# Gathers moved amid an expert pair's gate/up products, wider value products in two attention stages, and a later overflow loop in a hybrid decoder block

## The chip, the cores and the metric

The kernel runs on one core of a Trainium2 chip. A core has five engines with instruction streams of their own: TensorE (PE: matrix products and transposes), VectorE (DVE), ScalarE (ACT), GpSimd (POOL) and SyncE (SP, which here issues nearly all DMA transfers), and 16 DMA engines that move data between HBM and the on-chip memory SBUF. Products land in PSUM, eight banks of 2 KB a partition. Engines wait for one another on semaphores.

The metric is the device time of one execution in microseconds (us); lower is better.

## The reference

One decoder layer in float32, 512 tokens of width 1024, batch 1. Cut to what the change touches:

```python
h = rmsnorm(x, g_mix); proj = h @ w_in        # q, k, v of GLA and of MoBA, gates
o_g = gla_chunked(...)                        # 4 heads
o_m = moba_attention(q_m, k_m, v_m, rel_bias) # 8 heads of 64: softmax(q k^T + bias) @ v, causal
x = x + (sigmoid(z_g) * (o_g @ w_proj_gla) + sigmoid(z_m) * (o_m @ w_proj_moba)) @ w_out
k, v = split(mem_n @ w_ckv)                   # 256 memory tokens, 4 heads
x = x + memory_attention(rmsnorm(x, g_cross), mem_n, w_cq, w_ckv, w_co)
# hier_moe: 32 experts, each token goes to the top 2 of 8 in its best group
hid = silu(xb @ w_gate[e]) * (xb @ w_up[e])   # 1024 -> 512
out[token] += w * (hid @ w_down[e])           # 512 -> 1024
x = x + out; return rmsnorm(x, g_final)
```

Every expert is computed for up to 64 tokens at a fixed place; tokens beyond that go through a loop whose number of rounds is known only at run time. For these inputs it is zero.

## The kernel before

**Precision.** Most products keep float32 accuracy by splitting both operands into a high and a low part of 32 bits that TensorE takes in one pass; `mm3` issues three matmuls (high by high, low by high, high by low). `mm` is a single call; with plain float32 operands it leaves two records in the trace for each call. `wnext` hands out the next load of a weight list, split into high and low on ScalarE (L212) and VectorE (L213); a load is 512 KB.

**Ahead of the experts.** The input products run in the order of the list `plan`. `in_feat` makes features by tokens (`fo`), `in_rows` tokens by features (`ro`): for GLA's values `vg`, MoBA's values `vm`, and the memory's values `vc`. `in_rows` is called twice for each of them, for 256 columns at a time, with two loads a call of four 128-row parts each, and ScalarE evicts each tile of 128 tokens. The input products are woven with the GLA branch (`project`, `weave`). Then MoBA is woven with the gate projections (`gates`, the fill): for each of 16 items (four head pairs `hp` by four query tiles `i` of 128) the two scores `s_ps`; the values `mo_ps` of the item before; some fill; the softmax's end on VectorE (`normalise`); more fill; and the transposes of the probabilities (`ptp`, copied by ScalarE to `pt`). The table `FILL` says how much fill stands in either gap. `values` makes 2 (i + 1) products for the item, each 128 queries wide, onto 64 columns of the array for one head and the other 64 for the other.

**The experts.** 16 pairs of experts, p = 0 to 15. The pair's code runs for k = 0 to 7 `gate_up` (four calls, 128 by 64 tiles, two experts side by side), then `hidden` (silu on ScalarE, L1228; its product with up and the weight on VectorE, L1229), `hidden_t` (four transposes and a copy), and `down` for four parts, then `rows_hilo` splits the result. Between `hidden` and `down` stand the combine of the pair before (`c_ps`: 16 calls that add its results to the tokens' rows) and a part of a gather. `gather` picks the tokens of four experts, that is of two pairs, with a 0/1 matrix `oh` (`group_hots`, VectorE) in eight steps k of eight products (`g_ps`, 128 by 128 tiles), each evicted by ScalarE into `xT`; pair 2g − 2 runs four of these steps and pair 2g − 1 the other four, so all of a group's features are there before its first pair starts. `slot_rows` makes the matrix and the weights of the combine from the token codes that `c_bcast` copies to all partitions, by 16 transposes (`cb_ps`) amid pair 0.

**Loads of expert weights.** 384 loads of 512 KB, 24 a pair, into 48 buffers of one pool (`blk`, shared with `xT`, `oh` and others), issued by SP in order by `eload(n)`, which issues up to load n. A load waits until the products that read its buffer's last content are done, and no more than eight are under way. In pair p the kernel asks for 24 p + `DEPTH` loads at the start, two more behind every second k, and two more behind each part of `down`; `D0` gives the same for pair 0, and `elimit` holds the last 16 back until the loop has been passed.

**The loop.** `overflow` stands ahead of pair 15. It reads its round count into a register of every engine (L1266) and is entered and left through a barrier of all engines (L1268), also for zero rounds.

**The end.** The final norm works per tile of 128 tokens in two halves: VectorE makes the right, ScalarE (L1389) the left, and SP issues both output transfers (L1388, L1390).

## Time and profile before

| | us |
|---|---|
| three runs | 985.1, 985.75, 986.44 (median 985.75) |
| profiled execution, its own time | 985.1 |
| its span in the trace | 983.3 |
| TensorE busy | 961.1 |
| stages: projections and GLA | to about 183 |
| MoBA with the gates | 183 to 302 |
| merge, memory attention, routing | to 499.89 |
| expert pairs, to the end of the last down product | 499.89 to 969.5 |
| last combine, final norm, output | to 983.3 |

The profile is one execution. Its page gives the share of each engine, the stage windows the same for a stretch, with DMA rate and the granted clock of TensorE (1.00 is the higher of its two levels), and the timelines single instructions. A TensorE record's duration is longer than its share of the engine, since records overlap: what one costs is the step from its start to the next one's.

### The profile page before, as it was taken

What the parts mean: (1) busy time and instruction counts of PE and PEld (TensorE: products, weight loads), DVE (VectorE), ACT (ScalarE), POOL (GpSimd) and SP (SyncE); (2) the same over time, 40 slices, a digit from 0 to 9 for tenths busy, and PEclk for the clock granted to TensorE, in tenths of its full rate; (3) what the DMA queues carried; (4) which work ended last, traced back from release to release, by engine and by line L of the source; (5) the groups of instructions that cost most, each with busy time, mean ns of one, the idle gap of its engine ahead of it and who ended that gap; (6) DMA issues with size and microseconds to landing.
All of it is one profiled execution on the core that took longest, in us unless ns stands there. A gap on an engine that the chain in (4) does not pass through costs nothing. (4 is left out here: it accounts for less than half of the span.)

```text
span 983.3 us, 13899 instructions
## 1 busy us (share of the span) xinstructions
PE 961.1 (98%) x5305; PEld 645.5 (66%) x5305; DVE 474.8 (48%) x1048; ACT 311.7 (32%) x631; POOL 32.7 (3%) x46
## 2 busy tenths in 40 slices
PE   9999999999999999999999999999999999999985
PEld 7889779888788888999844555544555554455432
DVE  6343863345555746566752543434453333444314
ACT  5452633445446424455521111111111111111003
POOL 3200010000000000000000000000000000000003
PEclk9999999999999999999999999999999999999998
DMA  9512347133133522644588999999999999999993
GB/s 300 160 44 58 71 65 193 44 86 86 60 133 129 176 81 67 198 190 196 200 331 329 409 408 409 409 409 408 409 409 409 409 408 409 409 409 409 409 383 148
DMA packets 117161, 252.52 MB, mean 257 GB/s; under 512 B 10310, under 2 KB 61795, under 8 KB 117092
## 3 DMA queue, kind: packets, MB, share of 16 engines
q1 hardware_dynamic: 117092, 251.60, 69.3%
q8 instruction: 43, 0.70, 0.3%
q14 instruction: 26, 0.21, 0.1%
HBM read 247.90 MB, written 3.67 MB: 256 GB/s over the span
## 5 line engine op out<-in xcount | busy, mean ns | idle before, releaser
L136 PE MATMUL gu_ps<-we,xT 128*64 128x512 f32 x1024 | 229.3, 597 | 5.1 <-PEq L1268 3.8
L136 PEld LDWEIGHTS gu_ps<-we,xT 128*64 128x64 f32 x1024 | 78.0, 138 | 150.5 <-issue 134.6
L213 DVE TENSOR_TENSOR wlo<-wraw,whi 128x1024 fp32r<-128x1024 f32 (+1 forms) x71 | 86.6, 1238 | 90.0 <-ACT whi L212 89.8
L136 PE MATMUL y_ps<-we,hid_t 128*64 128x512 f32 x512 | 114.2, 595 | 0.3 <-issue 0.3
L1229 DVE SCALAR_TENSOR_TENSOR hid<-hid,ws,gu_ps 128x512 f32<-128x512 f32 x16 | 11.9, 747 | 194.9 <-PE gu_ps L136 194.9
L1262 DVE TENSOR_TENSOR x<-c_ps,x 128x512 f32<-128x512 f32 x120 | 76.7, 685 | 38.9 <-PE c_ps L136 38.9
L131 PE MATMUL fo<-hTh,whi 128*128 128x512 f32 x224 | 90.5, 404 | 0.0
L133 PE MATMUL fo<-hTh,wlo 128*128 128x512 f32 x224 | 87.5, 391 | 0.0
L132 PE MATMUL fo<-hTl,whi 128*128 128x512 f32 x224 | 87.4, 390 | 0.0
L136 PEld LDWEIGHTS y_ps<-we,hid_t 128*64 128x64 f32 x512 | 36.3, 137 | 68.8 <-issue 55.7
L212 ACT ACTIVATE whi<-wraw 128x1024 fp32r<-128x1024 f32 (+2 forms) x73 | 74.5, 1043 | 1.9 <-DMA wraw<-in_w_in_dram 1.8
L1228 ACT ACTIVATE hid<-gu_ps 128x512 f32<-128x512 f32 x16 | 9.6, 597 | 197.5 <-PE gu_ps L136 197.5
L136 PE MATMUL g_ps<-oh,xrh 128*128 128x256 f32 x256 | 64.6, 293 | 1.7 <-DVE oh L1030 1.7
L136 PE MATMUL g_ps<-oh,xrl 128*128 128x256 f32 x256 | 61.6, 281 | 0.0
L136 PEld LDWEIGHTS g_ps<-oh,xrh 128*128 128x128 f32 x256 | 47.0, 189 | 14.9 <-PE gu_ps L136 9.7
L133 PE MATMUL ro<-whi,hTl 128*128 128x256 f32 (+1 forms) x192 | 55.4, 289 | 0.8 <-DVE hTl L333 0.8
L131 PE MATMUL ro<-whi,hTh 128*128 128x256 f32 (+1 forms) x192 | 56.0, 291 | 0.0
L132 PE MATMUL ro<-wlo,hTh 128*128 128x256 f32 (+1 forms) x192 | 55.5, 289 | 0.2 <-POOL wlo L213 0.2
L212 ACT ACTIVATE yh<-y_ps 128x512 fp32r<-128x512 f32 x32 | 19.1, 598 | 109.9 <-PE y_ps L136 109.9
L136 PE MATMUL c_ps<-yh,ot 128*128 128x512 f32 x128 | 50.8, 397 | 0.7 <-ACT yh L212 0.7
L136 PE MATMUL c_ps<-yl,ot 128*128 128x512 f32 x128 | 50.8, 397 | 0.2 <-DVE yl L213 0.2
L131 PEld LDWEIGHTS fo<-hTh,whi 128*128 128x128 f32 x224 | 42.0, 188 | 12.0 <-issue 3.9
(320 smaller groups left out, 1544.5 us busy)
## 6 DMA issues: line engine op xcount, KB each, us to landing
we<-in_w_exp_gate_dram SPq DMA_DIRECT2D x128, 512.0 KB, 10.2
we<-in_w_exp_up_dram SPq DMA_DIRECT2D x128, 512.0 KB, 10.2
we<-in_w_exp_down_dram SPq DMA_DIRECT2D x128, 512.0 KB, 10.2
wraw<-in_w_in_dram SPq DMA_DIRECT2D x38, 512.0 KB, 3.8
wraw<-in_w_out_dram SPq DMA_DIRECT2D x8, 512.0 KB, 6.1
wraw<-in_w_ckv_dram SPq DMA_DIRECT2D x8, 512.0 KB, 4.6
wraw<-in_w_proj_gla_dram SPq DMA_DIRECT2D x4, 512.0 KB, 3.9
wraw<-in_w_proj_moba_dram SPq DMA_DIRECT2D x4, 512.0 KB, 4.3
```

Source lines behind the costliest of these rows:

```text
L131: PE.matmul(o, lh, rh, start=first, stop=False)
L132: PE.matmul(o, lh, rl, start=False, stop=False)
L133: PE.matmul(o, ll, rh, start=False, stop=last)
L136: PE.matmul(o, l, r, start=first, stop=last, **kw)
L212: S.activation(hi, src, AF.Copy)
L213: eng.tensor_tensor(lo, src, f(hi), op=ALU.subtract)
L1228: S.activation(row, gu[0][0:n], AF.Silu)
L1229: V.scalar_tensor_tensor(row, row, ws[:, 0:1], gu[1][0:n], op0=ALU.mult, op1=ALU.mult)
L1262: V.tensor_tensor(xs, o, xs, op=ALU.add)
```

## The change

- **Value rows 512 wide.** `in_rows` makes all 512 columns in one call, with four loads of two 128-row parts (`WIDE`) of the same size in place of two calls of two loads. Half the products, twice as wide; half the evictions, twice as wide.
- **MoBA values a head pair at a time.** `values(hp, pts)` runs once per head pair, behind the first scores of the next one, over all query tiles: for key tile j the queries from j on, 512, 384, 256 and 128 wide. `transposed` writes the probabilities of all four query tiles into two buffers a head, `pa` and `pb`, with one or two ScalarE copies a head.
- **The start.** The mean square of the second input tile moves from VectorE to ScalarE, into the gap that `to_feat` leaves for `between`.
- **`c_bcast`.** Its first two steps, the eight transposes of the codes, run ahead of the second half of the last gather before pair 0; the other two amid pair 0.
- **The gather.** A group's first four steps run behind the gate/up products of the odd pair ahead of it (p = 2g − 1), the other four amid the gate/up of its own first pair (p = 2g), one ahead of each k = 0 to 3. `xT` is taken from the pool in two halves; `group_hots` moves to k = 3 of the odd pair. Pair 0 runs no gather now and pair 14 runs four steps.
- **Loads.** `DEPTH` is 35 in pair 0 and 33 after it; `D0` is gone.
- **The loop.** The round count is read at the start of pair 14, and the loop stands in pair 15 ahead of k = 2 (`SPILL`); 372 loads are issued before it rather than 368. Inside it, products use one set of PSUM banks, `sp_ps`.
- **The end.** ScalarE issues the left halves' output transfers.

The diff, cut to its core:

```diff
-    def in_rows(n, evac, src, nt=NT, mark=None):
-        acc = [ps(f"ro{t}", [n]) for t in range(nt)]
-        for kh in range(2):
-            wh, wl = wnext(4, n)
+    def in_rows(evac, src, nt=NT, mark=None):
+        acc = [ps(f"ro{t}", [512]) for t in range(nt)]
+        kk = 0
+        for kn in WIDE:
+            wh, wl = wnext(kn, 512)
             for t in range(nt):
...
-    r1 = rms_scale(x_in[1], V)
-    to_feat(xr, hT, 0, lambda: wsplit(2))
+    def between():
+        r1.append(rms_scale(x_in[1]))
+        wsplit(2)
+    to_feat(xr, hT, 0, between)
...
-        def values(hp, i, pts, o_ps):
-            for j in range(i + 1):
+        def values(hp, pts):
+            o_ps = ps("mo_ps", [T])
+            for j in range(NT):
                 for half in range(2):
                     h = 2 * hp + half
                     sl = slice(64 * half, 64 * half + 64)
-                    mm(o_ps[sl, tcol(i)], vm[j][:, h * 64:(h + 1) * 64], pts[half][:, j, :], j == 0, j == i,
-                       skip_group_check=True)
+                    pa, pb = pts[half]
+                    p_j = pa[:, j, j * P:] if j < 2 else pb[:, j - 2, (j - 2) * P:]
+                    mm(o_ps[sl, j * P:], vm[j][:, h * 64:(h + 1) * 64], p_j, j == 0, j == NT - 1, skip_group_check=True)
...
             res = scores(hp, i)
-            if prev:
-                finish(*prev)
+            if prev and i == 0:
+                values(*prev)
...
+    bcast = c_bcast()
+    steps(bcast, 2)
     c_weights()
     c_gather(NT - 1)
...
-        if p == NP - 1:
-            eload(elimit[0])
-            overflow(*spilled)
-            elimit[0] = 12 * NE
-        eload(used + D0[0] if p == 0 else used + DEPTH)
-        if p % 2 == 0 and p:
-            xT = xT_next
+        depth = DEPTH[min(p, 1)]
+        if p == SPILL[0] - 1:
+            n_extra = nc.values_load(spilled[0][0:1, 0:1], ...
+        eload(used + depth)
         gu = [ps("gu_ps", [512]) for q in range(2)]
         s0 = (p % 2) * P
         for k in range(KD):
+            if (p, k) == SPILL[0:2]:
+                overflow(n_extra, *spilled)
+                elimit[0] = 12 * NE
+            if p % 2 == 0:
+                steps(gat, 1)
             gate_up(gu, k, [xT[k][:, s0 + CAP * i:s0 + CAP * i + CAP] for i in range(2)], w)
             if k % 2:
-                eload(D0[1 + k // 2] if p == 0 else used + DEPTH + 2 * (k + 1))
+                eload(used + depth + 2 * (k + 1))
...
+            if p % 2 and p + 1 < NP and k == OH_AT:
+                oh_next = group_hots((p + 1) // 2)
-        if p % 2 == 0 and p + 2 < NP:
-            xT_next = rows2("xT", KD, 4 * CAP)
-            gat = gather(oh_next, xT_next, 4 * CAP)
+        if p % 2 and p + 1 < NP:
+            xT = []
+            gat = gather(oh_next, xT, 4 * CAP)
...
-        gs = 4 if p + 2 < NP else 0
+        gs = 1 if p % 2 and p + 1 < NP else 0
...
-        SY.dma_start(out[tcol(t), 0:512], xg[t])
+        S.dma_start(out[tcol(t), 0:512], xg[t])
...
-SPILL_AT = 8
+WIDE = 2, 2, 2, 2
+SPILL = 15, 2, 372
...
-DEPTH = 30
-D0 = 34, 37, 41, 44, 47
+DEPTH = 35, 33
+OH_AT = 3
```

How the order moves, at three places. First TensorE's stream from the end of pair 1's down products into pair 2, before (`y_ps` down, `gu_ps` gate/up, `g_ps` gather, 16 calls leave 32 records):

```order
L136 MATMUL y_ps<-we,hid_t 64x512 x16
L136 MATMUL gu_ps<-we,xT_5124 64x512 x16
L136 MATMUL gu_ps<-we,xT_5125 64x512 x16
L136 MATMUL g_ps<-oh,xrh_4067 128x256
L136 MATMUL g_ps<-oh,xrl_4071 128x256
L136 MATMUL g_ps<-oh,xrh_4068 128x256
L136 MATMUL g_ps<-oh,xrl_4072 128x256
L136 MATMUL g_ps<-oh,xrh_4069 128x256
L136 MATMUL g_ps<-oh,xrl_4073 128x256
L136 MATMUL g_ps<-oh,xrh_4070 128x256
L136 MATMUL g_ps<-oh,xrl_4074 128x256
```

and after:

```order
L136 MATMUL y_ps<-we,hid_t 64x512 x16
L136 MATMUL g_ps<-oh,xrh_3812 128x256
L136 MATMUL g_ps<-oh,xrl_3816 128x256
L136 MATMUL g_ps<-oh,xrh_3813 128x256
L136 MATMUL g_ps<-oh,xrl_3817 128x256
L136 MATMUL g_ps<-oh,xrh_3814 128x256
L136 MATMUL g_ps<-oh,xrl_3818 128x256
L136 MATMUL g_ps<-oh,xrh_3815 128x256
L136 MATMUL g_ps<-oh,xrl_3819 128x256
L136 MATMUL gu_ps<-we,xT_4950 64x512 x4
```

The four gather steps of the next group that stood behind the gate/up products of an even pair are gone from there; one step of the pair's own group now stands ahead of each of the first four k.

Second, TensorE in MoBA where the fourth query tile of the first head pair is scored, before (`ptp` transposes, `s_ps` scores, `mo_ps` values, `fo` fill):

```order
L679 MATMUL ptp<-keep,pr 128x128 x6
L136 MATMUL s_ps<-km_1039,qm_1304 128x512 x2
L136 MATMUL s_ps<-km_1040,qm_1304 128x512 x2
L136 MATMUL mo_ps<-pt,vm_1518 64x128 x4
L136 MATMUL mo_ps<-pt,vm_1519 64x128 x2
L131 MATMUL fo<-hTh_145,whi 128x512
L132 MATMUL fo<-hTl_149,whi 128x512
```

and after, there and one item later, where the next head pair's first tile is scored:

```order
L675 MATMUL ptp<-keep,pr 128x128 x6
L136 MATMUL s_ps<-km_936,qm_1201 128x512 x2
L136 MATMUL s_ps<-km_937,qm_1201 128x512 x2
L131 MATMUL fo<-hTh_145,whi 128x512
L132 MATMUL fo<-hTl_149,whi 128x512
L133 MATMUL fo<-hTh_145,wlo 128x512
```

```order
L675 MATMUL ptp<-keep,pr 128x128 x8
L136 MATMUL s_ps<-km_989,qm_1309 128x256 x2
L136 MATMUL s_ps<-km_990,qm_1309 128x256 x2
L136 MATMUL mo_ps<-pa,vm_1415 64x512 x2
L136 MATMUL mo_ps<-pa,vm_1415 64x384 x2
L136 MATMUL mo_ps<-pb,vm_1416 64x256 x2
L136 MATMUL mo_ps<-pb,vm_1416 64x128 x2
L131 MATMUL fo<-hTh_145,whi 128x512
```

The values that stood behind every pair of scores stand behind the first scores of the next head pair alone, four widths for each head, and fill follows the other scores at once.

Third, TensorE around the loop, before, from pair 14's down products on:

```order
L136 MATMUL y_ps<-we,hid_t 64x512 x16
L1266 TENSOR_LOAD rt_xi
L1268 COMPARE_AND_BRANCH
L1268 UNCONDITIONAL_BRANCH
L1450 BRANCH_PREFETCH_HINT
```

and after, from the same products on:

```order
L136 MATMUL y_ps<-we,hid_t 64x512 x16
L136 MATMUL gu_ps<-we,xT_7467 64x512 x8
L1264 COMPARE_AND_BRANCH
L1264 UNCONDITIONAL_BRANCH
L1449 BRANCH_PREFETCH_HINT
```

The register load has moved out to the start of pair 14, and 8 calls of pair 15's gate/up, 16 records, stand between pair 14's down products and the loop's branch.

## Rows read from the trace of the kernel before

**Rows 1.** The first part of the page: busy time of each engine, its share of the span, and its instructions.

```profile
PE 961.1 (98%) x5305; PEld 645.5 (66%) x5305; DVE 474.8 (48%) x1048; ACT 311.7 (32%) x631; POOL 32.7 (3%) x46
```

**Rows 2.** The windows, two stretches of the MoE stage. Columns: the stretch; its length and TensorE's busy time with its instructions; weight loads, VectorE, ScalarE, GpSimd likewise; granted clock of TensorE; DMA share; GB/s.

```profile
534.00:900.00 366.00, 365.19 (x1873) 179.91 (x1870) 149.67 (x304) 54.17 (x101) 0.00 (x0) 1.00 1.03 409
940.00:945.00 5.00, 5.00 (x18) 1.84 (x16) 0.00 (x0) 0.00 (x0) 0.00 (x0) 0.67 1.00 363
```

**Rows 3.** The timeline of TensorE over pair 7. Columns, here and in the other timelines: start, duration, engine, line, operation, out<-in, tile, out shape, count of records, and in brackets an idle time before it with what ended it.

```profile
703.10 13.90 PE L136 MATMUL gu_ps<-we,xT 128*64 128x512 f32 x64
716.93 0.39 PE L136 MATMUL g_ps<-oh,xrh 128*128 128x256 f32 x1
...
718.91 0.60 PE L1235 MATMUL ht_ps<-keep,hid 128*128 128x128 f32 x4
719.26 0.36 PE L136 MATMUL g_ps<-oh,xrh 128*128 128x256 f32 x1
719.47 0.28 PE L136 MATMUL g_ps<-oh,xrl 128*128 128x256 f32 x1
...
720.30 0.40 PE L136 MATMUL c_ps<-yh,ot 128*128 128x512 f32 x1
...
725.07 7.09 PE L136 MATMUL y_ps<-we,hid_t 128*64 128x512 f32 x32
731.99 2.32 PE L136 MATMUL gu_ps<-we,xT 128*64 128x512 f32 x10
```

**Rows 4.** The timeline of TensorE over pairs 14 and 15.

```profile
907.90 11.32 PE L136 MATMUL gu_ps<-we,xT 128*64 128x512 f32 x50
...
923.67 0.50 PE L136 MATMUL c_ps<-yh,ot 128*128 128x512 f32 x1
...
928.01 7.09 PE L136 MATMUL y_ps<-we,hid_t 128*64 128x512 f32 x32
938.86 16.50 PE L136 MATMUL gu_ps<-we,xT 128*64 128x512 f32 x64 [3.77 <-PEq L1268]
955.29 0.50 PE L136 MATMUL c_ps<-yh,ot 128*128 128x512 f32 x1
...
967.57 1.94 PE L136 MATMUL y_ps<-we,hid_t 128*64 128x512 f32 x8
```

**Rows 5.** The groups of instructions by line and shape: busy time in all, mean ns of one, and the idle time of the engine before them with what ended it.

```profile
L136 PE MATMUL gu_ps<-we,xT 128*64 128x512 f32 x1024 | 229.3, 597 | 5.1 <-PEq L1268 3.8 <-DMA we<-in_w_exp_gate_dram 0.8 <-DMA we<-in_w_exp_up_dram 0.4
...
L1229 DVE SCALAR_TENSOR_TENSOR hid<-hid,ws,gu_ps 128x512 f32<-128x512 f32 x16 | 11.9, 747 | 194.9 <-PE gu_ps L136 194.9
...
L1228 ACT ACTIVATE hid<-gu_ps 128x512 f32<-128x512 f32 x16 | 9.6, 597 | 197.5 <-PE gu_ps L136 197.5
```

**Rows 6.** The timeline of SP's queue around the start of pair 15: when it issues loads of expert weights.

```profile
931.21 0.33 SPq L940 DMA_DIRECT2D we<-in_w_exp_up_dram  x1
938.72 0.33 SPq L940 DMA_DIRECT2D we<-in_w_exp_gate_dram  x1
```

**Rows 7.** The timeline of TensorE over the start of the MoE stage and the end of pair 0's combine stretch.

```profile
499.89 5.37 PE L136 MATMUL gu_ps<-we,xT 128*64 128x512 f32 x24
505.20 0.65 PE L1073 MATMUL cb_ps<-keep,rt_code 128*128 128x128 f32 x4
505.78 1.94 PE L136 MATMUL gu_ps<-we,xT 128*64 128x512 f32 x8
507.64 0.65 PE L1073 MATMUL cb_ps<-keep,rt_code 128*128 128x128 f32 x4
...
522.38 7.09 PE L136 MATMUL y_ps<-we,hid_t 128*64 128x512 f32 x32
```

**Rows 8.** The timeline of TensorE in the projections, two products of value rows 256 wide with 17 like them between.

```profile
83.73 0.28 PE L132 MATMUL ro<-wlo,hTh 128*128 128x256 f32 x1
...
85.89 0.28 PE L132 MATMUL ro<-wlo,hTh 128*128 128x256 f32 x1
```

**Rows 9.** The timeline of TensorE in the MoBA stage, fill products (fo) around transposes (ptp) and values (mo_ps).

```profile
190.26 0.66 PE L136 MATMUL mo_ps<-pt,vm 128*64 128x128 f32 x8
190.85 0.50 PE L131 MATMUL fo<-hTh,whi 128*128 128x512 f32 x1
191.18 0.39 PE L132 MATMUL fo<-hTl,whi 128*128 128x512 f32 x1
...
197.11 0.81 PE L679 MATMUL ptp<-keep,pr 128*128 128x128 f32 x6
...
207.46 1.57 PE L136 MATMUL mo_ps<-pt,vm 128*64 128x128 f32 x16
208.96 0.50 PE L131 MATMUL fo<-hTh,whi 128*128 128x512 f32 x1
209.30 0.39 PE L132 MATMUL fo<-hTl,whi 128*128 128x512 f32 x1
```

**Rows 10.** The tile mo_ps, its matmuls: count, shortest, middle and longest ns, first and last start, shape.

```profile
L136 PE MATMUL mo_ps<-pt,vm x160: 272/273/324, 183.0 to 301.2; 128*64 128x128 f32 x160
```

**Rows 11.** The timeline of VectorE, the end of the softmax whose transposes stand at 197.11 in rows 9.

```profile
196.70 0.42 DVE L672 TENSOR_SCALAR pr<-pr,ri 128x384 f32<-128x384 f32 x1
```

**Rows 12.** The timeline of SP's queue at the end: the last of the eight output transfers that it issues.

```profile
979.34 0.61 SPq L1390 DMA_DIRECT2D out_dram<-xg  x1
```

**Rows 13.** The timeline of ScalarE at the end, its last scaling of output rows.

```profile
976.61 1.33 ACT L1389 ACTIVATE xg<-xg,rr 128x512 f32<-128x512 f32 x2 [0.59 <-POOL rr L1382]
```

More of the change, by code (lines that the diff above doesn't have):

```diff
@@ L164, in steps @@
             next(g, None)
-    def chain(*gens):
-        for g in gens:
-            yield from g
     plan, loaded, ready, used = [], [], [], [0]
@@ L189, in block_kernel @@
     add_feat(w_in, 0, 2)
-    for j in range(2):
-        add_rows(w_in, 512 + 256 * j, 256)
+    add_rows(w_in, 512, 512, WIDE)
     add_feat(w_in, 2064, 4)
     add_feat(w_in, 1552, 4)
-    for j in range(2):
-        add_rows(w_in, 2576 + 256 * j, 256)
+    add_rows(w_in, 2576, 512, WIDE)
     add_feat(w_in, 3088, 16)
@@ L204, in block_kernel @@
     add_feat(w_cq, 0, 4)
-    for j in range(2):
-        add_rows(w_ckv, 512 + 256 * j, 256)
+    add_rows(w_ckv, 512, 512, WIDE)
     for c in range(2):
@@ L481, in project @@
         yield from in_feat(2, lambda i, o: S.activation(qk[i], o, AF.Copy, scale=0.125), hT, mark="qk")
-        for j in range(2):
-            yield from in_rows(256, lambda t, o: S.activation(vg[t][:, 256 * j:256 * j + 256], o, AF.Copy), hT)
-        marks.add("v")
+        yield from in_rows(lambda t, o: S.activation(vg[t], o, AF.Copy), hT, mark="v")
         yield from in_feat(4, keys, hT)
@@ L487, in project @@
         vm.extend(rows2("vm", NT))
-        for j in range(2):
-            yield from in_rows(256, lambda t, o: S.activation(vm[t][:, 256 * j:256 * j + 256], o, AF.Copy), hT)
+        yield from in_rows(lambda t, o: S.activation(vm[t], o, AF.Copy), hT)
     gla_out = []
@@ L709, in moba @@
             yield 0.64 * FILL[i][1]
-            prev = hp, i, transposed(i, res)
+            if i == 0:
+                prev = hp, [(blk("pa", [2, T]), med("pb", [2, 2 * P])) for half in range(2)]
+            transposed(i, res, prev[1])
         yield 1.0
-        finish(*prev)
+        values(*prev)
     fill = gates()
@@ L1078, in block_kernel @@
     xT = rows2("xT", KD, 4 * CAP)
-    vgen = chain(*(in_rows(256, lambda t, o, j=j: S.activation(vc[:, t, 256 * j:256 * j + 256], o, AF.Copy), mn, nt=2)
-                   for j in range(2)))
+    vgen = in_rows(lambda t, o: S.activation(vc[:, t, :], o, AF.Copy), mn, nt=2)
     c_scores(0)
@@ L1085, in block_kernel @@
     c_exp(1)
-    steps(vgen, 16)
+    steps(vgen, 8)
     c_normalise(0)
@@ L1263, in combine, with overflow @@
                 yield t, c
-    def overflow(xi, xb):
-        n_extra = nc.values_load(xi[0:1, 0:1], min_val=0, max_val=NX - 1,
-                                 skip_runtime_bounds_check_because="2 T assignments fill fewer than NX whole blocks")
+    def overflow(n_extra, xi, xb):
         with tc.For_i(0, n_extra, 1, iteration_sync='staggered') as i:
@@ L1281, in overflow @@
                 tile_hots(oh, rel, t, CAP, part)
-            drain(gather(oh, xT, CAP))
+            pb = [ps("sp_ps", [512]) for q in range(6)]
+            drain(gather(oh, xT, CAP, [b[:, 0:CAP] for b in pb[0:2]]))
             ot, ws = slot_rows(codes[0:CAP], CAP, oa)
             to = [blk("we", [2, 512]) for q in range(4)]
-            gu, load = [ps("gu_ps", [512]) for q in range(2)], load_gate_up(bass.ds(e, 1), to)
+            gu, load = pb[2:4], load_gate_up(bass.ds(e, 1), to)
             for j in range(4):
@@ L1289, in overflow @@
                     gate_up(gu, k, xT[k:k + 1], [{2 * j + q: w[q] for q in range(2)}])
-            hid_t = hidden_t(hidden(gu, ws, CAP, hid), CAP)
-            y_ps, load = [ps("y_ps", [512]) for c in range(2)], load_down(bass.ds(e, 1), to)
+            hid_t = hidden_t(hidden(gu, ws, CAP, hid), CAP, pb[4][:, 0:4 * CAP].rearrange("p (a n) -> p a n", a=4))
+            y_ps, load = pb[0:2], load_down(bass.ds(e, 1), to)
             for ft in range(4):
@@ L1295, in overflow @@
             for c in range(2):
-                drain(combine(ot, {c: rows_hilo(y_ps[c], CAP, parts)}))
+                drain(combine(ot, {c: rows_hilo(y_ps[c], CAP, parts)}, pb[2:6]))
     NP = NE // 2
-    bcast, slot, spill = c_bcast(), None, spill_list()
+    slot, spill = None, spill_list()
     comb, gat = iter(()), iter(())
-    xT_next = None
     for p in range(NP):
@@ L1304, in block_kernel @@
         used = 24 * p
-        if p == NP - 1:
-            eload(elimit[0])
-            overflow(*spilled)
-            elimit[0] = 12 * NE
-        eload(used + D0[0] if p == 0 else used + DEPTH)
-        if p % 2 == 0 and p:
-            xT = xT_next
+        depth = DEPTH[min(p, 1)]
+        if p == SPILL[0] - 1:
+            n_extra = nc.values_load(spilled[0][0:1, 0:1], min_val=0, max_val=NX - 1, skip_runtime_bounds_check_because=
+                                     "2 T assignments fill fewer than NX whole blocks")
+        eload(used + depth)
         gu = [ps("gu_ps", [512]) for q in range(2)]
@@ L1334, in block_kernel @@
         for i in range(3):
-            steps(gat, min(gs, 1))
+            steps(gat, gs)
             steps(comb, 2)
```

62 lines of the change are left out of this document (28 added, 34 removed).

## The prediction

> **What bounds the kernel now.** I read the page first: TensorE is busy for 961.1 us of a span of 983.3 [rows 1], so a change pays where it removes TensorE work or one of its few waits. The windows come next: from 534 to 900 us TensorE is busy for 365.19 us of 366, and the DMA engines move 409 GB/s, a share of 1.03 [rows 2]. Both are full there. One load of expert weights is 512 KB, so at that rate 512 KB / 409 GB/s = 1.28 us; 24 loads make a pair of experts, 30.8 us. TensorE's own pair is shorter [rows 3]: gate/up 703.10 to 716.93 = 13.83 us, four eighths of a gather, the combine and the hidden transposes to 725.07 = 8.14, down to 731.99 = 6.92, in all 28.89. So TensorE eats the loads' lead, pair by pair, and at the end it waits for them. The timeline of the last pairs shows where [rows 4]: gate/up of pair 14 takes 907.90 to 923.67 = 15.77 us, 1.94 over 13.83, and the line's group names waits for gate and up loads [rows 5]; ahead of pair 15 stands a gap of 3.77 us, released by the loop of L1268; and pair 15's gate/up takes 938.86 to 955.29 = 16.43, again 2.60 over. [...] The issue rows of the loads show what the loop does to DMA: 931.21, then 938.72, 7.51 us where the step was 1.28 [rows 6].
>
> The reader is to see two limits some microseconds apart. Whatever takes TensorE time away in the first 900 us is worth nothing unless the loads come earlier as well.
>
> **The MoE stage before, as a sum.** It starts at 499.89 [rows 7] and its last down products start at 967.57 and end 1.94 later, at 969.5 [rows 4]: 469.6 us. Without waits: pair 0 is 522.38 − 499.89 + 6.92 = 29.41 [rows 7]; pairs 1 to 13 are 13 × 28.89 = 375.6; pair 14, which has no gather, 13.83 + (928.01 − 923.67 = 4.34) + 6.92 = 25.09 [rows 3, 4]; pair 15, 13.83 + (969.5 − 955.29 = 14.2) = 28.05. In all 458.1, so 11.5 us are waits, all of them in the last four pairs.
>
> **Ahead of the MoE stage.** (a) Value rows 512 wide. 256 wide, the steps are 83.73 to 85.89 in 18, 0.120 us each [rows 8]; 26 products 512 wide of the same form take 191.18 to 197.11, 0.228 each [rows 9]. Two of 0.120 become one of 0.228: 0.012 saved in each of 192 for vg and vm and 48 for vc, 2.9 us. Loads keep their bytes; evictions on ScalarE become half as many and twice as wide, beside a TensorE that doesn't wait for them. (b) MoBA's values: 160 records of 128 columns now [rows 10]. An excursion of 8 takes 190.26 to 190.85 = 0.59, one of 16 takes 207.46 to 208.96 = 1.50 [rows 9]; on a line through both, 4 are 0.13 and 12 are 1.05, so a head pair is 3.3 us and the four 13.1. After it there are 16 records in a head pair, of 512, 384, 256 and 128 columns: at the 6.92 / 32 = 0.216 us of a down record of 512 [rows 3], in proportion, 4 × (0.216 + 0.162 + 0.108 + 0.07) = 2.2, with the entry about 2.5 (an estimate), so 10.0 in all. That saves 3.1, and 12 changes of shape fewer at about 0.1 (the first product behind values takes 208.96 to 209.30 = 0.34 in place of 0.228 [rows 9]), 4.2 together. Against it: a softmax has less TensorE work ahead of its transposes. Normalising the second head ended at 196.70 + 0.42 = 197.12, where the first head's transposes began at 197.11 [rows 9, 11]: some 0.3 us before the second head's, and the values that stood ahead of such a softmax, 0.59 for 8 records, are gone. The items later in the stage have more room, an item that starts a head pair gets more values ahead of it than now, and three or four are as close as this one; I take 1.2 us (0 to 4). Net 3.0. (c) The code transposes moved ahead of pair 0: eight at 0.58 for four (505.20 to 505.78 [rows 7]) are 1.2, and the two ScalarE copies stand ahead of those of the last gathered features; I take 1.5 later (1.1 to 2). (d) The square at the start on ScalarE in place of VectorE: one pass over a tile of rows changes engines while the first loads arrive; 0, with 0.4 either way (an estimate from the 0.75 of a VectorE pass half as wide [rows 5], most of it under the loads). Sum: the MoE stage starts 2.9 + 3.0 − 1.5 = 4.4 us earlier, at 495.5.
>
> **The MoE stage after.** What I need is the price of leaving gate/up for other products and coming back. Pair 0 shows it today: four transposes amid gate/up repeat every 507.64 − 505.20 = 2.44 us, of which 8 gate/up records are 8 × 0.216 = 1.73; 0.71 is an excursion of four transposes [rows 7]. Amid products of their own shape four take 718.91 to 719.26 = 0.35 [rows 3]; at the step of a gather record, twice as wide, they would take 0.47. So both edges together are 0.24 to 0.36; I take 0.31. The gather's 8 records are 0.118 each (719.47 to 720.30 in 7), 0.95 [rows 3].
> - Pair 0: 13.83 + 2 × 0.71 for the two weight transposes left in it = 15.3. No gather is there any more behind gate/up, so TensorE waits for silu 0.60, its product 0.75 [rows 5], the hidden transposes (0.65, as the four amid gate/up [rows 7]) and a copy like silu's 0.60: 2.6. With down 6.92: 24.8, 4.6 less than 29.41.
> - Seven odd pairs: as before, 28.89 each (four eighths of the gather behind gate/up): 202.2.
> - Seven even pairs: 25.09 as pair 14 today, four eighths 4 × 0.95 = 3.8, four excursions 4 × 0.31 = 1.2: 30.1 each, 210.7.
> - Pair 15: 28.05. The loop stands behind the products for k = 0 and 1, so TensorE has 16 × 0.216 = 3.46 us while the other engines reach the barrier; the gap was 3.77 with nothing ahead of it. That leaves 0.3 to 0.5, and 372 instead of 368 loads are issued before it. SP stops at the same barrier, DMA pauses for some 5 of the 6.2 us it does now, and the last loads are then about as late as TensorE wants them. With the register read at the start of pair 14: 1.0 (0 to 2.5).
> Sum: 24.8 + 202.2 + 210.7 + 28.05 + 1.0 = 466.8, 2.8 less than 469.6: 11.5 of waits go, 4.6 of pair 0 go, and pair 14's gather (3.8), 28 excursions (8.6) and the 1.0 come.
>
> Does DMA allow it? With 35 loads asked for at the start of the stage and the stream at 1.28 from about 4 us into it (an estimate: today's rows show that rate from 534, since a load waits for a slot before; the deeper limits and a pair 0 shorter by 4.6 free slots sooner), the last of 384 lands 4 + 349 × 1.28 = 451 us into the stage, or up to 5 later with the pause at the loop, and TensorE wants it about 7 before the end of the down products (half of the 32 records, 3.5, and the combine of the first half of the columns, about as long, come behind): 458 to 463. That is under 466.8, so TensorE sets the end and slots, not the rate, hold the loads.
>
> [...]
>
> **Tail.** SP issues all eight output transfers, the last at 979.34 for 0.61 us [rows 12], while ScalarE ends its last scaling at 976.61 + 1.33 = 977.94 [rows 13]. With ScalarE issuing four of them its chain ends near 979.2: 0.8 earlier (0.5 to 1.4). [...]
>
> **Sum.** 4.4 + 2.8 + 0.8 = 8.0. The profiled execution took 985.1 (span 983.3, 1.8 around it), 0.65 under the median of 985.75; on the median's basis 985.75 − 8.0 = 977.7.
>
> **The rivals.**
> - DMA sets the end: excursions are nearly free, or hidden. Then the stage is about 461 long, 5.8 less than my sum: 972. For: DMA is at a share of 1.03 for 366 us [rows 2], and the product behind a change of shape elsewhere loses only 0.11 [rows 9]. Against: the 0.71 in pair 0.
> - The waits come back. The loop still idles TensorE for most of 3.77 us with a granted clock of 0.67 behind it, or pair 0's idle 2.6 us is followed by a lower clock, or MoBA's softmax is exposed at its bound of 4 us: 3 to 6 us of the gain are lost, 980.5 to 983.7. For: the barrier needs every engine, the last of them VectorE behind the split of pair 14's products. Against: 3.46 us of products stand there.
> - Slower: a gather amid gate/up pays more than a transpose does, since its weights change with every record. It costs 28 × (price − 0.31); the gain of 8.0 is used up at 0.60, and from 0.67 on the kernel is slower by over 0.2%. If at both edges a whole gate/up record has to run out, 0.597 from start to end [rows 5] against its step of 0.216, the price is 2 × 0.38 = 0.76 and the time 977.7 + 12.6 = 990.3. Against: the transposes pay both edges too, 0.36 at most.
> - The change doesn't do what it says: gathers stay off the end of even pairs, but the loads run no deeper and pairs 12 to 14 wait as now, 5.1 us (11.5 less 3.77 for the gap and 2.60 behind it): 982.8. It is counted with the second.
>
> **How the numbers follow.** Forecast 977.7 with 0.55; DMA-bound 0.18; waits come back 0.15; no change 0.04; slower 0.08. Faster by over 0.2% (2 us, about what can be told from no change) is 0.55 + 0.18 + 0.15 = 0.88. The range reaches down to the DMA-bound end with a us of room, 970.5, and up into the second rival, 982.5; it leaves out the last of that and the two cases of no gain.
>
> **What would show it.** Right: pair 1's start about 25 us behind pair 0's; even pairs near 30.1 and odd ones near 28.9; no waits for loads in pairs 12 to 15; the gap at the loop under 1 us with a granted clock of 1.0 behind it; MoE starting near 495. Wrong: even pairs at 29 with waits for loads (DMA sets the end), or at 32 (excursions cost double); idle TensorE behind the scores in MoBA.

## The result and the profile after

| | before | after |
|---|---|---|
| median of the runs, us | 985.55 (4 runs, 985.1 to 986.44) | 977.58 (4 runs, 977.41 to 977.96) |
| ratio after to before, with its 95% interval | | 0.9919 [0.9901, 0.9936] |
| profiled execution, us | 985.1 | 977.96 |
| its span, us | 983.3 | 976.1 |
| expert stage begins | 499.89 | 493.22 |
| last down product ends | 969.5 | 962.3 |
| from there to the end of the span | 13.8 | 13.8 |

The kernel is faster by 8.0 us, and 977.7 was forecast. By stage the spans say something else than the sum of the prediction: of 7.2 us, 6.7 are won ahead of the expert stage (forecast 4.4), 0.5 in it (forecast 2.8) and nothing behind it (forecast 0.8). The other 0.8 of the 8.0 lies between the executions: the profiled one of before was 0.45 under its median, that of after 0.4 over.

The timeline of TensorE over pairs 7 and 8 of the kernel after, an odd and an even one, with the gather steps amid gate/up (the view of rows 3, now of the kernel after):

```profile
695.43 13.90 PE L136 MATMUL gu_ps<-we,xT 128*64 128x512 f32 x64
...
717.40 7.09 PE L136 MATMUL y_ps<-we,hid_t 128*64 128x512 f32 x32
724.42 0.39 PE L136 MATMUL g_ps<-oh,xrh 128*128 128x256 f32 x1
...
725.57 1.94 PE L136 MATMUL gu_ps<-we,xT 128*64 128x512 f32 x8
...
728.58 1.94 PE L136 MATMUL gu_ps<-we,xT 128*64 128x512 f32 x8
...
731.59 1.94 PE L136 MATMUL gu_ps<-we,xT 128*64 128x512 f32 x8
...
734.60 8.80 PE L136 MATMUL gu_ps<-we,xT 128*64 128x512 f32 x40
743.34 0.50 PE L136 MATMUL c_ps<-yh,ot 128*128 128x512 f32 x1
...
747.67 7.09 PE L136 MATMUL y_ps<-we,hid_t 128*64 128x512 f32 x32
754.59 1.89 PE L136 MATMUL gu_ps<-we,xT 128*64 128x512 f32 x8
```

The odd pair takes 695.43 to 724.42 = 29.0 us (28.9 before). In the even pair a step of the gather and 8 gate/up records repeat every 731.59 − 728.58 = 3.01 us; without 8 × 0.216 and 0.95 that leaves 0.33 for an excursion, where 0.31 was forecast. Odd and even together take 754.59 − 695.43 = 59.16; 58.99 was the sum's figure.

The start of the stage, TensorE (the view of rows 7):

```profile
489.86 1.19 PE L136 MATMUL g_ps<-oh,xrh 128*128 128x256 f32 x8 [1.40 <-DVE oh L1025]
490.89 1.03 PE L1068 MATMUL cb_ps<-keep,rt_code 128*128 128x128 f32 x8
491.68 1.20 PE L136 MATMUL g_ps<-oh,xrl 128*128 128x256 f32 x8
493.22 5.37 PE L136 MATMUL gu_ps<-we,xT 128*64 128x512 f32 x24 [0.35 <-ACT xT L1042]
...
509.57 0.66 PE L1233 MATMUL ht_ps<-keep,hid 128*128 128x128 f32 x4 [0.93 <-DVE hid L1227]
510.92 7.09 PE L136 MATMUL y_ps<-we,hid_t 128*64 128x512 f32 x32 [0.69 <-ACT hid_t L1235]
517.83 12.62 PE L136 MATMUL gu_ps<-we,xT 128*64 128x512 f32 x58
```

The wait of 1.40 for the 0/1 matrix is there as before, the eight code transposes stand behind it and cost 491.68 − 490.89 = 0.79, and 0.35 more goes to the features' copies, which ScalarE makes after those of the codes. Pair 0 takes 24.61 us (24.8 forecast), with its two waits of 0.93 and 0.69 and no drop of the granted clock.

The end of the stage, TensorE in pair 15 (the view of rows 4), then SP's issues around the loop (rows 6) and three windows (rows 2):

```profile
932.07 11.32 PE L136 MATMUL gu_ps<-we,xT 128*64 128x512 f32 x50
943.67 1.08 PE L136 MATMUL gu_ps<-we,xT 128*64 128x512 f32 x4 [0.28 <-DMA we<-in_w_exp_gate_dram]
945.43 2.79 PE L136 MATMUL gu_ps<-we,xT 128*64 128x512 f32 x10 [0.68 <-DMA we<-in_w_exp_up_dram]
...
960.37 1.94 PE L136 MATMUL y_ps<-we,hid_t 128*64 128x512 f32 x8
```

```profile
925.51 0.33 SPq L935 DMA_DIRECT2D we<-in_w_exp_up_dram  x1
935.24 0.33 SPq L935 DMA_DIRECT2D we<-in_w_exp_gate_dram  x1
...
937.81 7.97 SPq L941 DMA_DIRECT2D we<-in_w_exp_down_dram  x8
```

```profile
497.00:505.00 8.00, 8.00 (x40) 2.79 (x38) 1.68 (x5) 1.19 (x2) 0.00 (x0) 1.00 0.96 349
530.00:900.00 370.00, 370.00 (x1866) 175.81 (x1862) 152.52 (x313) 53.94 (x102) 0.00 (x0) 1.00 1.03 409
932.00:936.00 4.00, 4.00 (x22) 1.39 (x20) 1.39 (x2) 0.65 (x2) 0.00 (x0) 1.00 0.29 116
```

The bare gap of 3.77 us at the loop is gone, and with it the granted clock of 0.50 that the kernel before shows from 940 to 943 us: it is 1.00 in the window that holds the loop. Pair 15 still takes 932.07 to 962.3 = 30.2 us; it waits for a gate and an up load. The loads run at 409 GB/s from 530 to 900 us, as before, so they did not become free of their rate; SP issues the next load 9.7 us after the last, and the window from 932 to 936 shows DMA at 116 GB/s. The two loads that pair 15 waits for are among the twelve that the loop held back: the first of these is issued at 935.24.

The last load of the stage is the eighth of the row at 937.81. It is issued at 945.45 and lands at 955.57, and the last down product ends 6.74 us later, at 962.31. In the kernel before it lands at 962.77, and the last down product ends 6.74 us later as well, at 969.51. TensorE's weight loads for these products wait for that load, to 955.61 in the kernel after and to 962.81 before. So its landing sets the end of the stage in both kernels, and counted from the stage's begin it moved by 0.5 us only, from 462.9 to 462.4.

### The profile page after: what moved, and what is told of

Read it like the earlier page. It is cut to its first block, busy times and chain, and to the rows that moved or that the text cites. A ratio compares the mean times of both kernels' runs of the same rounds, so it can differ in the third digit from the quotient of the medians.

```text
span 976.1 us, 13247 instructions
## 1 busy us (share of the span) xinstructions
PE 956.1 (98%) x4969; PEld 622.3 (64%) x4969; DVE 471.6 (48%) x1047; ACT 312.4 (32%) x639; POOL 32.6 (3%) x46
## 4 chain that ended last, share of the span: by engine, by line
PE 92%; DVE 3%; ACT 3%; issue 1%; DMA 1%; SPq 0%; ACTq 0%; POOL 0%; DVEq 0%
PE gu_ps L136 22%; PE y_ps L136 12%; PE fo L131 7%; PE fo L132 7%; PE fo L133 7%; PE g_ps L136 7%; PE c_ps L136 6%; PE ro L133 2%; PE ro L131 2%; PE ro L132 2%; PE x2o L136 2%; PE xo L132 1%; PE xo L133 1%; PE xo L131 1%; PE o_ps L136 1%; PE mo_ps L136 1%
## 5 line engine op out<-in xcount | busy, mean ns | idle before, releaser
L136 PEld LDWEIGHTS gu_ps<-we,xT 128*64 128x64 f32 x1024 | 70.9, 137 | 135.3 <-issue 121.8
L1200 ACT ACTIVATE xT<-g_ps,gfeat 128x256 f32<-128x256 f32 x56 | 25.8, 474 | 89.2 <-PE g_ps L136 57.6
L131 PEld LDWEIGHTS fo<-hTh,whi 128*128 128x128 f32 x224 | 42.1, 188 | 10.1 <-issue 1.9
L133 PEld LDWEIGHTS fo<-hTh,wlo 128*128 128x128 f32 x224 | 42.0, 188 | 9.1
L136 PEld LDWEIGHTS g_ps<-oh,xrl 128*128 128x128 f32 x256 | 47.1, 189 | 0.6
```

Of the source, the lines that this page charges most:

```text
L131: PE.matmul(o, lh, rh, start=first, stop=False)
L133: PE.matmul(o, ll, rh, start=False, stop=last)
L136: PE.matmul(o, l, r, start=first, stop=last, **kw)
L1200: S.activation(xT[k], o, AF.Copy, scale=gfeat[:, k:k + 1])
```

## The experiments

Each kernel was timed beside the kernel before on the same chip, so ratios are compared; 0.0010 is about 1 us.

| | what | median, us | ratio to before |
|---|---|---|---|
| | the change | 977.58 | 0.9919 [0.9901, 0.9936] |
| e1 | before, with the parts ahead of the expert stage | 978.18 | 0.9932 [0.9918, 0.9945] |
| e11 | before, with MoBA's values alone | 980.95 | 0.9959 [0.9945, 0.9972] |
| e12 | before, with the value rows alone | 982.98 | 0.9974 [0.9964, 0.9985] |
| e2 | after, one excursion in place of four | 974.0 | 0.9889 [0.9874, 0.9904] |
| e3 | after, gather and load limits as before | 976.79 | 0.9916 [0.9902, 0.9929] |
| e4 | after, loop at the start of pair 15 | 982.77 | 0.9978 [0.9969, 0.9987] |
| e5 | after, whole gather behind odd pairs | 991.44 | 1.0053 [1.0034, 1.0072] |
| e6 | after, SP issues all outputs | 978.33 | 0.9924 [0.9911, 0.9937] |
| e7 | e2 with the loop ahead of k = 4 | 974.76 | 0.9895 [0.9881, 0.991] |
| e8 | e7 with the codes amid pair 0 | 974.72 | 0.9886 [0.9872, 0.9901] |
| e9 | e2 with the codes amid pair 0 | 972.75 | 0.9872 [0.9857, 0.9887] |
| e10 | e9 with 37 loads asked for at the start | 972.27 | 0.9868 [0.9853, 0.9883] |

The theory ahead of them: both limits, TensorE and the loads, meet at the end of the changed kernel; nearly all of the gain comes from ahead of the expert stage, and in it the loop's new place pays for the excursions. The rivals: TensorE alone, or the loads alone, set the end.

**e1: only the parts ahead of the expert stage.** The hunks of `in_rows`, `values`, `transposed` and `between`, put on the kernel before:

```diff
-    def in_rows(n, evac, src, nt=NT, mark=None):
+    def in_rows(evac, src, nt=NT, mark=None):
...
-        def values(hp, i, pts, o_ps):
+        def values(hp, pts):
...
-    r1 = rms_scale(x_in[1], V)
+        r1.append(rms_scale(x_in[1]))
```

> The kernel before with only the parts ahead of the expert stage changed: value rows 512 wide, MoBA's values a head pair at a time, the square at the start on ScalarE. The expert stage, its loads, the loop and the end stay as they were. Theory: in the changed kernel the expert stage begins 6.67 us earlier (493.22 for 499.89) although the code transposes cost about 1.1 there, and the stage itself is only half a microsecond shorter (469.1 for 469.6), so nearly all of the change's 8 us comes from these parts: 985.55 - 7.7 = 977.9, 977.3 to 978.6. Rival: the load stream sets the end of the kernel before, and an earlier start of TensorE only waits longer for loads: 981 to 984.

978.18. The stage begins at 492.62 and the last down product ends 470 us later, as long as in the kernel before: what is won ahead of the stage goes through whole, since its loads begin with it (the last one lands 463.2 us into the stage, 462.9 before). It is 1.3 us behind the full change, less than the two intervals can tell apart. The rival falls.

**e11 and e12: the two attention parts alone.** Of e1's hunks e11 has these, and e12 the first two lines of e1's:

```diff
-        def values(hp, i, pts, o_ps):
+        def values(hp, pts):
...
-            if prev:
-                finish(*prev)
+            if prev and i == 0:
+                values(*prev)
```

> The kernel before with MoBA's values alone changed. Theory: from the first score to the first product behind MoBA the kernel before takes 301.38 - 177.0 = 124.4 us and the changed one 294.07 - 174.3 = 119.8; 4.6 less, all of it through to the end: 985.2 - 4.6 = 980.6. Rival: the term of the prediction, 3.0: 982.2.

> The kernel before with the value rows alone 512 wide. Theory: the term of the prediction, 0.012 us for each of 240: 2.9, all of it through to the end: 985.2 - 2.9 = 982.3. Rival: GLA's chunks, which stand between these products, wait for values that come in one piece: 983.5 to 985.

The stage begins at 495.49 with the values alone, 4.4 earlier, and at 497.05 with the value rows alone, 2.8 earlier. The ratios give 4.0 and 2.6 us, in sum 6.6, and e1's 6.7. Both theories hold; for the values the forecast's 3.0 still lies inside the interval (2.8 to 5.4), but not at the stage's begin.

**e2: one excursion.**

```diff
-            if p % 2 == 0:
-                steps(gat, 1)
+            if p % 2 == 0 and k == 0:
+                steps(gat, 4)
```

> The changed kernel with the four gather steps of an even pair together ahead of k = 0, in place of one ahead of each of k = 0 to 3: 7 excursions where there were 28. Theory: three excursions fewer a pair at 0.36 us each (29.02 - 25.09 - 3 x 0.95 over three) free 7.6 us of TensorE, of which the loads, that run at their full rate to 925 us now, let through about half: the loop is passed earlier, so their pause there goes, and the last load lands some 4 us earlier. 973.8, 972.5 to 975.5. Rival one: excursions cost next to nothing, or loads alone set the end: 977 to 978. Rival two: TensorE alone sets the end: 970.

974.0. An odd and an even pair take 33.02 + 25.14 = 58.16 us, 1.00 less than 59.16, so one excursion fewer gives 0.33: 7.0 us in the seven even pairs. The time fell by 3 to 3.6, the stage by 3.7. The rest of the 7.0 went into loads: pair 13 takes 0.6 us more than its like and pair 15 2.75 more than in the kernel after, with 3.1 us of waits for loads that TensorE's timeline names:

```profile
925.66 8.10 PE L136 MATMUL gu_ps<-we,xT 128*64 128x512 f32 x34
935.49 1.08 PE L136 MATMUL gu_ps<-we,xT 128*64 128x512 f32 x4 [1.73 <-DMA we<-in_w_exp_gate_dram]
...
940.58 1.08 PE L136 MATMUL gu_ps<-we,xT 128*64 128x512 f32 x4 [1.01 <-DMA we<-in_w_exp_gate_dram]
```

Neither single-limit rival gives this time: excursions are real time on TensorE, 0.33 us each, and the landing of the loads sets the end. What links the two is the loop. It is passed 6.3 us earlier than in the kernel after, so SP's step between the two loads around it is 3.06 us (925.87 to 928.93) in place of 9.73, and the last load lands 3.7 us earlier, 458.7 us into the stage.

**e3: the gather and the limits of the loads as before.** Two sets of `xT` are held again; all else as after:

```diff
-            if p % 2 == 0:
-                steps(gat, 1)
...
-        if p % 2 and p + 1 < NP:
-            xT = []
-            gat = gather(oh_next, xT, 4 * CAP)
+        if p % 2 == 0 and p + 2 < NP:
+            xT_next = rows2("xT", KD, 4 * CAP)
+            gat = gather(oh_next, xT_next, 4 * CAP)
...
-        gs = 1 if p % 2 and p + 1 < NP else 0
+        gs = 1 if p + 2 < NP else 0
...
-DEPTH = 35, 33
+DEPTH = 30
+D0 = 34, 37, 41, 44, 47
```

> The changed kernel with the gather, the buffers and the limits of the loads as in the kernel before: four steps behind the gate/up products of every pair up to 13, features of a whole group held while the next are made, 30 loads ahead. Loop, tail, code transposes and attention stages stay changed. Theory: TensorE's work in the expert stage falls by 8.6 us of excursions to about 458, but the loads come later, since the limits and buffers of before let them reach full rate only 34 us into the stage: with load 367 issued 431.3 us into it and 16 more at 1.28, the end is that of the loads, 469 us, and the time 977 to 979.5. Rival: TensorE sets the end in the changed kernel, and without excursions it is 966 to 970.

976.79, a little under the range's lower end. No even pair has an excursion, pairs 4 to 11 take 28.89 each, and pairs 12 to 15 wait for loads again (pair 12 29.86, pair 13 30.74). Its ratio can't be told from the change's: the part that names the change, the gather amid gate/up with deeper loads, is worth nothing that these runs can measure. What it wins by earlier loads it loses at the loop: load 372, the last ahead of the loop, is issued 432.3 us into the stage, 433.9 in e3, but then SP stands for 9.7 us, 3.1 in e3, since TensorE with its excursions gets there later.

**e4: the loop back at the start of pair 15.**

```diff
-SPILL = 15, 2, 372
+SPILL = 15, 0, 368
```

> The changed kernel with the loop back at the start of pair 15, with 368 loads issued ahead of it; the round count is still read at the start of pair 14. Theory: the barrier is again bare: TensorE stands for about 3.3 us (3.77 less the register read), the granted clock falls behind it for another 1.7, and the wait of 2.25 us that pair 15 has now goes into that: 977.6 + 3 = 980.6, 979.5 to 982.5. Rival: the loads set the end and pause at the barrier in either place, so the place is worth under 1 us: 977.5 to 978.6.

982.77, a little over the range's upper end: 5.8 us by the ratios, 4.7 by the profiled executions. TensorE's row at the loop, the window behind it, and SP's two issues around the loop:

```profile
935.58 17.34 PE L136 MATMUL gu_ps<-we,xT 128*64 128x512 f32 x64 [3.19 <-PEq L1264]
```

```profile
935.00:945.00 10.00, 9.42 (x32) 3.20 (x34) 0.00 (x0) 0.00 (x0) 0.00 (x0) 0.68 0.83 288
```

```profile
919.89 0.33 SPq L935 DMA_DIRECT2D we<-in_w_exp_up_dram  x1
935.38 0.33 SPq L935 DMA_DIRECT2D we<-in_w_exp_gate_dram  x1
```

The gap is back, and the granted clock is 0.68 over the ten microseconds behind it (1.00 in the same stretch of the kernel after). But the edit brings back a second thing: 16 loads stand behind the loop in place of 12. The first of them is issued 442.0 us into the stage in both kernels (935.38 and 935.24). The last one lands 4.6 us later than in the kernel after, and the last down product again ends 6.74 us behind it, so the trace has the whole 4.6 us in the loads. What the gap and the clock cost by themselves was not tried. The rival's price, under 1 us, falls; its premise, that the loads set the end and pause in either place, fits the traces.

**e5: the whole gather behind odd pairs.**

```diff
-            if p % 2 == 0:
-                steps(gat, 1)
...
-        gs = 1 if p % 2 and p + 1 < NP else 0
+        gs = 2 if p % 2 and p + 1 < NP else 0
```

> The changed kernel with all eight steps of a gather behind the gate/up products of the odd pair ahead of its group, two at a time among the combine, and none amid gate/up: no excursion at all. Theory: beside e2 this frees another 7 x 0.30 us of TensorE, but there the load stream already decides (pair 15 waited 3.2 us for loads), so it gives nothing more: 974, 973.3 to 975. Rival one: TensorE still decides: 972. Rival two: the long stretch of an odd pair in which no buffer comes free starves the loads: over 975.5.

991.44, and none of the three: nothing starves (DMA runs at 411 GB/s there), yet every odd pair but the first takes 36.36 in place of 28.89 + 4 × 0.95 = 32.7. TensorE's timeline near the end of an odd pair's combine, and two windows:

```profile
846.93 0.50 PE L136 MATMUL c_ps<-yh,ot 128*128 128x512 f32 x1 [0.78 <-DVE x L1260]
...
848.45 0.38 PE L136 MATMUL g_ps<-oh,xrh 128*128 128x256 f32 x1 [0.78 <-DVE x L1260]
```

```profile
846.00:849.00 3.00, 1.44 (x7) 0.85 (x7) 1.38 (x2) 0.00 (x0) 0.00 (x0) 1.00 1.03 411
849.00:853.00 4.00, 4.00 (x19) 3.32 (x17) 0.58 (x1) 1.43 (x4) 0.00 (x0) 0.57 1.04 411
```

TensorE waits twice 0.78 us for VectorE, which adds the combine's tiles to the tokens' rows and has to free their PSUM banks; then the granted clock is 0.57 on the mean of the next 4 us. The two waits stand in all seven odd pairs, 1.6 us each time; the clock fell behind them in six. In pair 1, with the same two waits (to 541.16 and 542.67), it stayed at 1.00, and the pair took 34.85, 1.5 less than the others. So what two such waits cost varies, and the single runs spread from 984.8 to 994.7.

**e6: all outputs issued by SP.**

```diff
-        S.dma_start(out[tcol(t), 0:512], xg[t])
+        SY.dma_start(out[tcol(t), 0:512], xg[t])
```

> The changed kernel with all eight output transfers issued by SP, as before. Theory: in the traces of before and after the last transfer lands 12.75 and 12.78 us after the last split on ScalarE began, though the last issue came 0.7 us earlier; 2 MB at the 380 GB/s that the end shows are 5.5 us from the first issue on, so the bytes decide and the issuing engine doesn't: 977.6 within 0.4. Rival, as predicted: the second issuing engine is worth 0.8: 978.4.

0.9924 against 0.9919: no difference to be seen. The windows of the 6.8 us up to the last landing, of the kernel before and of the one after:

```profile
975.50:982.30 6.80, 0.00 (x0) 0.00 (x0) 2.16 (x5) 1.86 (x3) 1.51 (x2) 0.64 0.83 308
```

```profile
968.30:975.10 6.80, 0.00 (x0) 0.00 (x0) 2.14 (x4) 2.16 (x3) 1.44 (x2) 0.52 0.83 308
```

308 GB/s over the same 6.8 us in both, though the last issue ended 0.7 us earlier after than before, counted from the end of the span. In the middle of the stretch the DMA engines are full: a share of 1.03 and 380 GB/s (978 to 980 before, 970 to 972 after). So the bytes decide from the first issue on; the issuing engine doesn't.

**e7 and e8: the loop later, and the codes back.** On e2, the first hunk for e7, all for e8:

```diff
-SPILL = 15, 2, 372
+SPILL = 15, 4, 376
...
-    steps(bcast, 2)
...
-                if k == BC_AT + 1:
+                if k == BC_AT + 3:
```

> The kernel of e2 with the loop ahead of k = 4 of pair 15 and 376 loads issued before it. Theory: the loads set the end there; they paused at the loop for 3.06 us where their step is 1.28 (925.87 to 928.93), and with four more products pairs ahead of the barrier TensorE reaches it after SP: the pause goes and 1.8 us with it: 972.2, 971.5 to 973. Rival: SP reaches the barrier after TensorE, which then stands: 974 to 975.5.

> The kernel of e7 with all four steps of the code transposes amid pair 0, as before. Theory: the expert stage starts 1.1 us earlier, pair 0 is 1.4 longer; where the loads decide, the start of the stage counts, since buffers come free from there on, and pair 0's two excursions do not: 1.1 less than e7, 971.1. Rival: TensorE in pair 0 decides how fast buffers come free: 0 to 0.5 more than e7.

974.76 and 974.72: no better than e2. TensorE's timeline of pair 15 in e7, SP's issues around the loop, and the instruction queues in the DMA view from 930 to 940 us:

```profile
925.07 7.50 PE L136 MATMUL gu_ps<-we,xT 128*64 128x512 f32 x32
932.85 1.83 PE L136 MATMUL gu_ps<-we,xT 128*64 128x512 f32 x4 [0.28 <-PEq L1264]
937.61 6.23 PE L136 MATMUL gu_ps<-we,xT 128*64 128x512 f32 x28 [2.93 <-issue]
```

```profile
929.80 0.33 SPq L935 DMA_DIRECT2D we<-in_w_exp_up_dram  x1
932.86 8.40 SPq L941 DMA_DIRECT2D we<-in_w_exp_down_dram  x8
```

```profile
q14 instruction: 3, 0.02, 0.7%
q8 instruction: 1, 0.02, 0.7%
```

The theory of e7 fails: SP's step at the loop is 3.06 us (929.80 to 932.86), the same as in e2, so the pause did not go. The barrier costs TensorE 0.28 us; but four records behind the loop TensorE stands for 2.93 us that the profile puts on "issue", on no semaphore and no load. The loads go on at 365 to 416 GB/s in that stretch, and four transfers of instructions fall between 930 and 940 us. The kernel after has four in the same window and no such wait, and e3 and e4, where TensorE stands at the barrier as well (0.27 and 3.19 us), show none either. What TensorE waited for in those 2.93 us was not shown. In e7's profile the wait cost next to nothing, since the loads weren't there either: the last down product ends 6.74 us behind the last load, as in e2. In e8's, where the wait is 3.32, the granted clock is 0.50 behind it (937 to 943 us; 1.00 in e7), so that 29 gate/up records take 9.32 us there and 28 in e7 6.16, and the last down product ends 10.1 us behind the last load, the one profile in which TensorE and not the loads sets the end. The runs of the two kernels lie between 973.2 and 976.4, so this may differ from run to run.

**e9 and e10: the codes back on e2, then more loads at the start.** e9 has the last two hunks of e8 on e2, e10 also this:

```diff
-DEPTH = 35, 33
+DEPTH = 37, 33
```

> The kernel of e2 (loop ahead of k = 2, 372 loads before it) with all four steps of the code transposes amid pair 0, as before. [...] Where the loads decide, the 0.84 counts and pair 0 doesn't: 973.2 for the 974.0 of e2. Rival: pair 0's length decides when buffers come free: 974 to 974.8.

> The kernel of e9 with 37 instead of 35 loads asked for at the start of pair 0, and two more all through it. Theory: the loads set the end and move only 249 to 349 GB/s in the first 12 us of the stage, for want of requests; two loads more at 1.28 us each are up to 2.5 us, of which buffers that are not yet free take some: 1 less than e9, 972.2. Rival: buffers decide and not the limit: the same as e9.

972.75 and 972.27. e9 is 1.7 us under e2 by the ratios, less than the two intervals can tell apart. In the traces its stage begins 0.7 us earlier (492.51 for 493.25) and its last load lands 2.2 earlier (949.70 for 951.92), while pair 0 is 1.5 longer. That the start counts and pair 0 doesn't fits, but it explains 0.7 of the 2.2 only; the rest stays open. The 0.84 that the expectation counts is by how much e8's stage begins before e7's; of the waits behind the loop in those two, 2.93 and 3.32 us, only e8's came through to the end of the stage. Two loads more add 0.4, inside the noise, and here the rival fits: the last load lands 457.2 us into the stage in e9 and 457.3 in e10. Both are faster than the kernel before and than the change. In e10 pair 15 still waits for loads (TensorE's timeline):

```profile
925.46 11.51 PE L136 MATMUL gu_ps<-we,xT 128*64 128x512 f32 x50
938.01 1.08 PE L136 MATMUL gu_ps<-we,xT 128*64 128x512 f32 x4 [1.04 <-DMA we<-in_w_exp_gate_dram]
939.30 2.79 PE L136 MATMUL gu_ps<-we,xT 128*64 128x512 f32 x10 [0.21 <-DMA we<-in_w_exp_up_dram]
```

**The last load in all traces.** In us into the stage, when the last of the 384 loads lands and when the last down product ends:

| | last load lands | last down product ends |
|---|---|---|
| before | 462.9 | 469.6 |
| the change | 462.4 | 469.1 |
| e2 | 458.7 | 465.4 |
| e3 | 460.0 | 466.8 |
| e4 | 466.9 | 473.7 |
| e7 | 457.7 | 464.5 |
| e8 | 458.2 | 468.3 |
| e9 | 457.2 | 463.9 |
| e10 | 457.3 | 464.0 |

In all but e8 the second is 6.7 us behind the first, and so it is in e1, e5, e6, e11 and e12.

## Why the prediction was right, and where it was not

The time, 977.58, lies 0.1 from the forecast, and that is partly luck: its terms missed by +2.3, −2.3 and −0.8 us, and the difference between the profiled executions made up the rest.

- **Value rows**, 2.9: right (2.6 by e12's ratio, 2.8 by the stage's begin).
- **MoBA's values**, 3.0: the mechanism right, the term mis-sized; 4.0 by e11's ratio and 4.4 by the stage's begin. The step that failed is the exposed softmax at 1.2. TensorE's timeline of the item before a head pair's end and of one without values:

```profile
201.86 0.63 PE L675 MATMUL ptp<-keep,pr 128*128 128x128 f32 x4 [0.35 <-DVE sm L666]
202.65 0.63 PE L675 MATMUL ptp<-keep,pr 128*128 128x128 f32 x4 [0.16 <-DVE pr L669]
...
203.67 1.79 PE L136 MATMUL mo_ps<-pa,vm 128*64 128x512 f32 x8
205.23 0.89 PE L136 MATMUL mo_ps<-pb,vm 128*64 128x256 f32 x8
206.05 0.50 PE L131 MATMUL fo<-hTh,whi 128*128 128x512 f32 x1
...
211.08 0.72 PE L136 MATMUL s_ps<-km,qm 128*128 128x256 f32 x4
211.64 0.40 PE L131 MATMUL fo<-hTh,whi 128*128 128x512 f32 x1
```

  The values of a head pair take 203.67 to 206.05 = 2.4 us, as forecast (2.5), and an item without them goes on from its scores to the fill in 0.56. Transposes do wait for VectorE, 0.9 us in all (0.35 + 0.16 here), but the 0.7 us that values waited for ScalarE's copies of the probabilities, in the waits of the kernel before, are gone with them: net 0.2, where 1.2 was taken.
- **The code transposes**, 1.5 later: the timeline has 0.79 and 0.35, but a stage without them ahead begins only 0.6 to 0.8 earlier (0.60 in e1 against the change, 0.74 in e9 against e2, 0.84 in e8 against e7). The term was sized too high.
- **The square at the start**, 0: nothing to be seen. e1's stage begins 7.27 earlier, of which e11 and e12 explain 4.40 and 2.84.
- **Pair 0**, 24.8: 24.61. **Odd and even pairs**, 58.99: 59.16. The price of an excursion, taken from transposes that stood amid gate/up before, held for gathers: 0.33 for 0.31. This rules out the slower rival, which needed 0.67. One reading of the kernel before was a little off: of its 11.5 us of waits 0.4 stand in pair 2 (29.30 us) and not in the last four.
- **Pair 15 and the loop**, 29.05: 30.2. The gap and the lower clock went as forecast, and e4 shows that they come back with the old place. But the step "TensorE sets the end and slots, not the rate, hold the loads" failed: the loads run at 409 GB/s through the stage, and the last of them sets its end, 6.74 us before the last down product ends (about 7 was forecast). The term that was wrong is the landing of that load: 451 to 456 us into the stage by the forecast, 462.4 measured. Load 368 landed 437.3 us into the stage, where the same sum gives 4 + 333 × 1.28 = 430.2, so 7 us were missing ahead of the loop. 4.5 of them were missing at load 72 already (55.9 for 51.4): in the first 12 us of the stage the loads move 349 GB/s and less (249 in the window 493 to 497, 349 in 497 to 505). The pause at the loop took 4.5 more, where up to 5 was forecast. The deeper limits did bring load 368 4.5 us ahead of the kernel before (441.9), but then SP stood for 9.7 us at the loop, 7.5 before, until the other engines were there, and nearly all of it was lost again. So the rival "DMA sets the end" had the mechanism, and its 972 rested on the same early estimate. TensorE's time counts through the moment at which it comes to the loop: of the 7.0 us that e2 took from it 3.7 came through in the stage.
- **The tail**, 0.8: nothing. The last issue ended 0.7 earlier and the last landing wasn't earlier; the step took the issue for what ended last, where it was the transfer of 2 MB from the first issue on.

## What to carry to other kernels

Where two streams are both full, find the one that ends last before you count a microsecond of the other: here the last product stands 6.7 us behind the last load, before and after the change. TensorE's savings count only where they let the loads go on earlier (7 us give 3 to 4, by way of the loop at which the loads wait), loads that run further ahead win nothing if they are stopped for TensorE later (load 368 landed 4.5 us earlier, the last one 0.5), and what happens ahead of both goes through whole (e1). Group work of another tile shape into as few excursions as its deadline allows (0.33 us each here); but look at the engine that empties its PSUM banks first, since two waits of 0.78 us made a pair 3.7 us longer where the clock fell to 0.57 behind them (e5). When a stretch ends with transfers, ask whether their bytes or their issues end last before moving the issues.

## What the runs showed of the hardware that was not expected

- Two waits of 0.78 us within 3 us were followed by a lower granted clock in six odd pairs of e5 (0.57 over the 4 us from 849 to 853) and by none in the seventh, pair 1 (1.00); pair 0's waits of 0.93 and 0.69, 0.7 us of work apart, were followed by none either (1.00, kernel after).
- Behind the exit of a loop that ran no round TensorE stood for 2.93 us in e7 and 3.32 in e8 without a semaphore or a load to wait for, but not in e3 and e4; the granted clock behind it was 0.50 in e8's profile and 1.00 in e7's.
- Going from 128 by 64 tiles to 128 by 128 and back came out at 0.24 to 0.36 us for four transposes (kernel before) and at 0.33 for eight gather products (kernel after).
